# Expert index look-up in three wide VectorE instructions, and query-weight low parts moved from GpSimd to VectorE

## The chip, the cores and the metric

The kernel runs on one core of one Trainium2 chip. The metric is device time in microseconds (us): the median of three runs is 3392.26 us (3391.84 to 3396.86). In the profile PE is the matrix engine (TensorE), PEld its weight loads, DVE is VectorE, ACT is ScalarE, POOL is GpSimd, and SP is the queue that issues most DMAs.

## The reference, cut to what matters

The program is a two-block transformer over 512 tokens of width 1024 in fp32. The first block mixes attention, a recurrent layer and a routed feed-forward layer; the second ends in a sparse feed-forward layer with 16384 experts, each a row `u` and a row `v` of 1024 numbers. Only that last layer is touched. For each of 8 heads it does this:

```python
q = (xb @ w_query).reshape(128, 8, 2, 128)
sc = einsum('thpd,hpkd->thpk', q, sub_keys)             # 2 x 128 scores per head
s_top, i_top = top_k(sc, 16)                            # for each of the two halves
cand = s_top[:, :, 0, :, None] + s_top[:, :, 1, None, :]
cand_idx = i_top[:, :, 0, :, None] * 128 + i_top[:, :, 1, None, :]
best, pos = top_k(cand, 16)                             # 16 ranks out of the pair sums
eidx = take_along_axis(cand_idx, pos, axis=-1)          # <- the look-up
g = softmax(best)
h = gelu(einsum('thkd,td->thk', expert_u[eidx], xb))
out = einsum('thk,thkd->td', g * h, expert_v[eidx])
```

## The kernel before

The last phase (`phase_d`, L1064) has four stretches: a norm, the query stage (`d_query`, L1177), the gates (`d_gates`, L1245) and a main loop over 128 blocks of 128 experts (L1132).

*Query stage.* A loop over 8 groups g, one for each head. For each group two blocks of query weights (`wq`, 128x1024) are loaded. Each is split by `split` (L1053): ScalarE rounds it to the matrix engine's format (`wqh`, L1058), and an engine given as `eng` makes the low part `wql` = `wq` - `wqh` (L1061). Before the change that engine is GpSimd, with one buffer for `wqh` and one for `wql`. TensorE does 24 matmuls for each block (L1192), ScalarE copies the result (`qT`, L1194), 8 small matmuls (L1201) make the scores `sc`, and VectorE takes the top 16 of each row with five instructions of `top16` (L1285); GpSimd turns the found indices into floats (`it`, `pos`, L1294). VectorE adds the pair sums (`cd`) and GpSimd makes the matching expert numbers (`ci`), 50 candidates a token (L1216, L1218). A second `top16` gives `best` and `pos`. Then comes the look-up, L1222 to L1227: for each of 4 token tiles and 16 ranks, one VectorE instruction compares a row 0 to 49 with the rank's position, multiplies by `ci` and sums along the row into `ei`. The chip runs it as two instructions, the operation and the reading of the accumulator.

*Work beside it.* `h_step` (L1080) makes expert scores for one block of 128 experts: a load `uraw`, a split into `uh` (ScalarE) and `ul` (GpSimd, 128x1024, L1061), 24 matmuls (L1088), and a GELU `G` on ScalarE. In the code the first 33 of these (LA, L1066 and L1105) stand behind the gates. They need nothing of the query stage.

*Gates and main loop.* `d_gates` needs `ei` and the softmax of all groups. It builds a dense weight table with 768 matmuls, shared between VectorE, GpSimd and ScalarE, and stores it as `w_d`. The main loop reads it back as `wb`, and in each step does 18 matmuls (L1146), one later `h_step`, and gathers and sums for the last 128 tokens.

*Order.* Each engine runs its own queue in order. The order in each queue is made when the program is built, by a planner that simulates the timeline with a cost for each instruction (L1307). Only the VectorE queue of the main loop is in the order of the code (L1131). So the instructions of several groups, and `h_step` blocks, stand interleaved in the queues.

Of the kernel before, what the change touches and what calls it, by code (L numbers as in the profile page):

```python
# [5 lines left out]
F32 = mybir.dt.float32  # L6
# [4 lines left out]
OP = mybir.AluOpType  # L11
AX = mybir.AxisListType
# [11 lines left out]
NCAND = len(CANDS)  # L24
# [133 lines left out]
class K:  # L158
# [1018 lines left out]
    def d_query(self, dq, ps, hh, hl):  # L1177
        nc, I, X, C = self.nc, self.I, self.X, self.C
        sub = dq.tile([128, 16, 128], F32, name="sub")
        nc.sync.dma_start(sub, I["subk"])  # L1180
        best = dq.tile([128, 4, 8, 16], F32, name="best")
        for g in range(8):
            qT = dq.tile([128, 2, 512], F32, name="qT", bufs=2)
            for j in range(2):
                w = dq.tile([128, 8, 128], F32, name="wq", bufs=3)
                nc.sync.dma_start(w.rearrange("p k c -> p (k c)"), I["w_q"][2 * g + j])
                wh, wl = self.split(dq, "wq", w, [128, 8, 128], bufs=1, eng=nc.gpsimd)
                p = ps.tile([128, 512], F32, name="pj", tag="pj")
                n = 0
                for k in range(8):  # L1190
                    for l, r in ((wh, hh), (wh, hl), (wl, hh)):
                        nc.tensor.matmul(p, l[:, k, :], r[:, k, :], start=(n == 0), stop=(n == 23))  # L1192
                        n += 1
                nc.scalar.copy(qT[:, j, :], p)  # L1194
            st = dq.tile([128, 4, 2, 16], F32, name="st", bufs=2)
            it = dq.tile([128, 4, 2, 16], F32, name="it", bufs=2)
            for half in range(2):
                p = ps.tile([128, 2, 2, 128], F32, name="psc", tag="tr")
                for t in range(2):
                    for j in range(2):  # L1200
                        nc.tensor.matmul(p[:, t, j, :], qT[:, j, (2 * half + t) * 128:(2 * half + t) * 128 + 128],  # L1201
                                         sub[:, 2 * g + j, :], start=True, stop=True)
                sc = dq.tile([128, 2, 2, 128], F32, name="sc", bufs=2)
                nc.scalar.copy(sc, p)
                for t in range(2):
                    for j in range(2):
                        self.top16(dq, sc[:, t, j, :], st[:, 2 * half + t, j, :], it[:, 2 * half + t, j, :], 128)
            cd = dq.tile([128, 4, NCAND], F32, name="cd", bufs=2)
            ci = dq.tile([128, 4, NCAND], F32, name="ci", bufs=2)
            i1 = dq.tile([128, 4, 16], F32, name="i1", bufs=2)  # L1210
            nc.gpsimd.tensor_scalar(i1, it[:, :, 0, :], 128.0, None, op0=OP.mult)
            for a, b2, dst, eng in ((st[:, :, 0, :], st[:, :, 1, :], cd, nc.vector), (i1, it[:, :, 1, :], ci, nc.gpsimd)):
                o = 0
                for i in range(8):
                    n = 16 // (i + 1)
                    eng.tensor_add(dst[:, :, o:o + n], b2[:, :, 0:n], a[:, :, i:i + 1].to_broadcast([128, 4, n]))  # L1216
                    o += n
                eng.tensor_add(dst[:, :, o:o + 8], a[:, :, 8:16], b2[:, :, 0:1].to_broadcast([128, 4, 8]))  # L1218
            pos = dq.tile([128, 4, 16], F32, name="pos", bufs=2)
            for t in range(4):  # L1220
                self.top16(dq, cd[:, t, :], best[:, t, g, :], pos[:, t, :], NCAND)
            for t in range(4):  # L1222
                for k in range(16):
                    eq = dq.tile([128, NCAND], F32, name="eq", bufs=2)
                    nc.vector.scalar_tensor_tensor(eq, C("iota")[:, 0:NCAND], pos[:, t, k:k + 1], ci[:, t, :],
                                                   op0=OP.is_equal, op1=OP.mult,
                                                   accum_out=self.ei[:, t, g * 16 + k:g * 16 + k + 1])  # L1227
        eu, ev = self.eix
        nc.vector.tensor_copy(eu, self.ei[:, 3, :])
        hi = dq.tile([128, 128], I32, name="ehi")  # L1230
        nc.vector.tensor_scalar(hi, eu, 7, None, op0=OP.logical_shift_right)
        nc.vector.tensor_scalar(ev, eu, 127, None, op0=OP.bitwise_and)
        nc.vector.tensor_scalar(ev, ev, 7, None, op0=OP.logical_shift_left)
        nc.vector.tensor_add(ev, ev, hi)
        bf = best.rearrange("p t h k -> p (t h) k")
        g3 = self.gt.rearrange("p t (h k) -> p (t h) k", h=8)
        nc.vector.tensor_sub(g3, bf, bf[:, :, 0:1].to_broadcast([128, 32, 16]))
        nc.scalar.activation(g3, g3, AF.Exp)
        sm = dq.tile([128, 32], F32, name="smg")
        nc.vector.tensor_reduce(sm, g3, axis=AX.X, op=OP.add)  # L1240
        nc.vector.reciprocal(sm, sm)
        nc.vector.tensor_mul(g3, g3, sm.unsqueeze(2).to_broadcast([128, 32, 16]))
        nc.gpsimd.tensor_copy(self.g3, self.gt[:, 3, :])
# [67 lines left out]
```

## Time and profile before

| | |
|---|---|
| median of the runs | 3392.26 us |
| span of the profiled execution, first to last instruction | 3389.1 us |
| median less span | 3.2 us |
| TensorE busy in the span | 3087.1 us (91%) |
| VectorE | 1869.1 us (55%) |
| ScalarE | 972.4 us (29%) |
| GpSimd | 1147.7 us (34%) |
| mean granted TensorE clock | 0.966 |

The page gives the span of the profiled execution, and no other time of its own. An engine's busy time is the union of its instructions' times. One instruction's recorded time can overlap that of the next on the same engine, so mean times are longer than the distance from start to start. The shares are averages over very different stretches of the program; the stretch that the change touches runs from about 1996 to 2310 us of the span.

### The profile page before, as it was taken

The page shows a single profiled execution, that of the slowest core. Times are in us where ns is not written, and L with a number is a line of the kernel's source. Part 1 is how long each engine was busy: PE and PEld are TensorE (multiplying, and loading weights), DVE is VectorE, ACT ScalarE, POOL GpSimd, SP SyncE. Part 2 cuts the span into 40 slices and gives each one's busy share as a digit, 9 for nine tenths or more (in the row PEclk, how much of TensorE's full clock was granted, in tenths as well). Part 3 has the DMA queues.
Part 4 walks back from the last instruction along what each step waited for, and adds up shares of the span by engine and source line. Part 5 has one row for each costly group of instructions (what it writes and reads, how often), then busy time and mean ns, then how long its engine had stood idle before and what let it go on. Part 6 is the DMA issues. An engine that isn't in the chain of part 4 may idle for free. (4 is left out here: it accounts for less than half of the span.)

```text
span 3389.1 us, 43135 instructions
## 1 busy us (share of the span) xinstructions
PE 3087.1 (91%) x16081; PEld 2175.6 (64%) x16081; DVE 1869.1 (55%) x4502; ACT 972.4 (29%) x1745; POOL 1147.7 (34%) x979
## 2 busy tenths in 40 slices
PE   7999999978988888888879998878889999999998
PEld 6777776463323323333356677767779999999986
DVE  2456665460000000000043649999979988898978
ACT  3333333220000000000033642226833333333332
POOL 0433321010000000000012134447858877777743
PEclk9999999989999999999988999988999999999999
DMA  4221112488999999999931252215788888888877
GB/s 145 100 73 60 57 67 85 136 322 349 428 426 427 427 428 426 427 427 428 420 103 64 69 171 82 69 57 165 206 305 314 314 292 306 300 300 303 291 258 265
DMA packets 193358, 837.91 MB, mean 247 GB/s; under 512 B 16509, under 2 KB 66301, under 8 KB 168446
## 3 DMA queue, kind: packets, MB, share of 16 engines
q1 hardware_dynamic: 153230, 693.52, 53.4%
q0 software_dynamic: 38592, 140.53, 11.8%
q8 instruction: 127, 2.08, 0.2%
q10 hardware_dynamic: 1328, 1.11, 0.1%
q14 instruction: 81, 0.66, 0.1%
HBM read 794.47 MB, written 40.63 MB: 246 GB/s over the span
## 5 line engine op out<-in xcount | busy, mean ns | idle before, releaser
L876 DVE TENSOR_TENSOR sg<-sg,pu 128x512 f32<-128x512 f32 x32 | 22.0, 687 | 681.9 <-PE pu L872 681.9
L1061 POOL TENSOR_TENSOR ul<-uraw,uh 128x1024 fp32r<-128x1024 f32 x128 | 333.4, 2606 | 124.6 <-ACT uh L1058 123.2
L1088 PE MATMUL ph<-hTh,ul 128*128 128x384 f32 x1024 | 347.9, 340 | 20.7 <-POOL ul L1061 20.7
L1088 PE MATMUL ph<-hTh,uh 128*128 128x384 f32 x1024 | 348.5, 341 | 0.4 <-ACT G L1091 0.4
L1088 PE MATMUL ph<-hTl,uh 128*128 128x384 f32 x1024 | 348.0, 340 | 0.0
L1146 PE MATMUL pY<-vh,ah 128*128 128x512 f32 x768 | 302.5, 394 | 20.3 <-ACT ah L1058 20.3
L1146 PE MATMUL pY<-vl,ah 128*128 128x512 f32 x768 | 300.4, 391 | 0.0
L872 PE MATMUL pu<-wt,xeT 128*64 128x512 f32 x1024 | 259.9, 611 | 33.5 <-DMA wt<-in_wu_dram 33.5
L1146 PE MATMUL pY<-vh,al 128*128 128x512 f32 x768 | 278.3, 389 | 0.0
L872 PE MATMUL pg<-wt,xeT 128*64 128x512 f32 x1024 | 256.4, 610 | 21.2 <-DMA wt<-in_wg_dram 21.2
L885 PE MATMUL pd<-wt,aT 128*64 128x512 f32 x1024 | 245.2, 597 | 22.6 <-ACT aT L881 22.6
L306 PE MATMUL pj<-hh,wh 128*128 128x512 f32 x528 | 216.0, 409 | 1.8 <-DVE hl L205 1.1
L306 PE MATMUL pj<-hh,wl 128*128 128x512 f32 x528 | 217.2, 411 | 0.0
L306 PE MATMUL pj<-hl,wh 128*128 128x512 f32 x528 | 215.0, 407 | 0.0
L853 POOL DMA_INDIRECT xe<-h_d,idi x8 | 7.6, 955 | 612.2 <-PE pt L859 578.9
L1088 PEld LDWEIGHTS ph<-hTh,ul 128*128 128x128 f32 x1024 | 194.6, 190 | 23.5 <-POOL ul L1061 23.1
L872 PEld LDWEIGHTS pu<-wt,xeT 128*64 128x64 f32 x1024 | 85.7, 141 | 192.3 <-issue 145.3
L1058 ACT CAST vh<-vraw 128x1024 fp32r<-128x1024 f32 x128 | 134.6, 1051 | 258.9 <-PE pY L1146 212.9
L872 PEld LDWEIGHTS pg<-wt,xeT 128*64 128x64 f32 x1024 | 86.5, 140 | 180.4 <-issue 148.0
L1088 PEld LDWEIGHTS ph<-hTh,uh 128*128 128x128 f32 x1024 | 195.0, 191 | 5.7 <-ACT G L1091 1.1
L1088 PEld LDWEIGHTS ph<-hTl,uh 128*128 128x128 f32 x1024 | 194.9, 190 | 4.4
L885 PEld LDWEIGHTS pd<-wt,aT 128*64 128x64 f32 x1024 | 89.5, 136 | 151.0 <-issue 120.2
(434 smaller groups left out, 6287.0 us busy)
## 6 DMA issues: line engine op xcount, KB each, us to landing
wt<-in_wg_dram SPq DMA_DIRECT2D x64, 2048.0 KB
wt<-in_wu_dram SPq DMA_DIRECT2D x64, 2048.0 KB
wt<-in_wd_dram SPq DMA_DIRECT2D x64, 2048.0 KB
uraw<-in_put_dram SPq DMA_DIRECT2D x128, 512.0 KB
vraw<-in_pv_dram SPq DMA_DIRECT2D x128, 512.0 KB
wraw<-in_w_in_dram SPq DMA_DIRECT2D x32, 1024.0 KB
w_d<-wst SPq DMA_DIRECT2D x12, 2048.0 KB
wb<-w_d SPq DMA_DIRECT2D x32, 768.0 KB
```

The source lines that it names most:

```text
L306: nc.tensor.matmul(p, l[:, k, :], r[:, k, :], start=(i == 0), stop=(i == 23))
L853: nc.gpsimd.indirect_dma_start(out=xe, out_offset=None, in_=h_d, in_offset=bass.IndirectOffsetOnAxis(ap=idi[:, p:p + 1], axis=0))
L872: nc.tensor.matmul(dst[e * 64:e * 64 + 64], xT[:, k, e * 64:e * 64 + 64], ww[e][:, k, :], start=(k == 0), stop=(k == 7))
L876: nc.vector.tensor_mul(sg, sg, pu)
L885: nc.tensor.matmul(pd[h][e * 64:e * 64 + 64], aT[:, k, e * 64:e * 64 + 64], wd[e][:, k, h * 512:h * 512 + 512], start=(c == 0 and k == 0), ...
L1058: nc.scalar.copy(hi, src)
L1061: (eng or nc.vector).tensor_sub(lo, src, hi)
L1088: nc.tensor.matmul(p, l[:, k, :], r[:, k, 0:ND], start=(n == 0), stop=(n == 23))
L1146: nc.tensor.matmul(pY[t][h], l[:, t * 128:t * 128 + 128], r[:, h * 512:h * 512 + 512], start=(s == 0 and n == 0), stop=(s == 127 and n == 2))
```

## The change

The look-up of one token tile is done for all 16 ranks at once, over a tile of 16x50: a comparison of the row 0 to 49 (repeated for each rank) with the 16 positions (each repeated 50 times), a product with `ci` (repeated for each rank), and a sum along the last axis. The tile `eq` has one buffer of 800 floats a partition, where it had two of 50. Second, the low parts `wql` are made by the default engine of `split`, VectorE, and `wqh` and `wql` have two buffers each.

```diff
@@ d_query, for each of 8 groups and 2 blocks
-                wh, wl = self.split(dq, "wq", w, [128, 8, 128], bufs=1, eng=nc.gpsimd)
+                wh, wl = self.split(dq, "wq", w, [128, 8, 128], bufs=2)
@@ d_query, for each of 8 groups
             for t in range(4):
-                for k in range(16):
-                    eq = dq.tile([128, NCAND], F32, name="eq", bufs=2)
-                    nc.vector.scalar_tensor_tensor(eq, C("iota")[:, 0:NCAND], pos[:, t, k:k + 1], ci[:, t, :],
-                                                   op0=OP.is_equal, op1=OP.mult,
-                                                   accum_out=self.ei[:, t, g * 16 + k:g * 16 + k + 1])
+                eq = dq.tile([128, 16, NCAND], F32, name="eq")
+                nc.vector.tensor_tensor(eq, C("iota")[:, None, 0:NCAND].to_broadcast([128, 16, NCAND]),
+                                        pos[:, t, :].unsqueeze(2).to_broadcast([128, 16, NCAND]), op=OP.is_equal)
+                nc.vector.tensor_mul(eq, eq, ci[:, t:t + 1, :].to_broadcast([128, 16, NCAND]))
+                nc.vector.tensor_reduce(self.ei[:, t, g * 16:g * 16 + 16], eq, axis=AX.X, op=OP.add)
```

## Rows read from the trace of the kernel before

**Rows 1.** Stretches (us from:to, length): busy PE, PEld, DVE, ACT, POOL; clock, DMA, GB/s.
```profile
2024.00:2310.00 286.00, 230.58 (x1132) 207.03 (x1130) 284.44 (x1880) 73.83 (x104) 131.24 (x219) 0.91 0.22 71
2310.00:2464.00 154.00, 120.20 (x849) 108.36 (x848) 131.73 (x466) 121.49 (x320) 135.29 (x202) 0.93 0.69 201
2464.00:3389.00 925.00, 911.41 (x4512) 815.96 (x4512) 814.41 (x775) 325.99 (x441) 629.46 (x340) 0.99 0.84 296
```
**Rows 2.** VectorE, 2024 to 2310: busy us, mean ns, idle before, releaser.
```profile
L1225 DVE SCALAR_TENSOR_TENSOR eq<-con,pos,ci 128x50 f32<-128x50 f32 x512 | 183.4, 398 | 0.7 <-POOL ci L1218 0.7
```
**Rows 3.** Line L1225: ns least, median, most; first and last start.
```profile
L1225 DVE SCALAR_TENSOR_TENSOR eq<-con,pos,ci x512: 169/259/2531, 2040.3 to 2307.2; 128x50 f32<-128x50 f32 x171
L1225 DVE DVE_READ_ACCUMULATOR eq<-con,pos,ci x512: 70/76/84, 2042.7 to 2307.4; 128x1 f32 x171
```
**Rows 4.** Timeline, VectorE (start, us): first and last of 16 looks.
```profile
2117.51 0.26 DVE L1225 SCALAR_TENSOR_TENSOR eq<-con,pos,ci 128x50 f32<-128x50 f32 x1
...
2120.38 0.26 DVE L1225 SCALAR_TENSOR_TENSOR eq<-con,pos,ci 128x50 f32<-128x50 f32 x1
```
**Rows 5.** Timeline, VectorE, 2104 to 2114 us.
```profile
2104.23 2.33 DVE L1225 SCALAR_TENSOR_TENSOR eq<-con,pos,ci 128x50 f32<-128x50 f32 x1
...
2111.80 0.20 DVE L1290 FIND_INDEX8 iu<-best,cd 128x8 uint32<-128x50 f32 x1
...
2112.10 1.86 DVE L1225 SCALAR_TENSOR_TENSOR eq<-con,pos,ci 128x50 f32<-128x50 f32 x1
```
**Rows 6.** Timeline, GpSimd, the same stretch.
```profile
2104.09 2.40 POOL L1061 TENSOR_TENSOR ul<-uraw,uh 128x1024 fp32r<-128x1024 f32 x1
...
2111.55 2.34 POOL L1061 TENSOR_TENSOR wql<-wq,wqh 128x1024 fp32r<-128x1024 f32 x1
```
**Rows 7.** GpSimd groups, 2024 to 2310.
```profile
L1061 POOL TENSOR_TENSOR ul<-uraw,uh 128x1024 fp32r<-128x1024 f32 x27 | 64.2, 2380 | 6.6 <-ACT uh L1058 6.6
L1061 POOL TENSOR_TENSOR wql<-wq,wqh 128x1024 fp32r<-128x1024 f32 x13 | 30.7, 2364 | 0.0
```
**Rows 8.** Timeline, VectorE: instructions of 512 elements, and a next one.
```profile
2281.37 0.68 DVE L1240 TENSOR_REDUCE smg<-gt 128x32 f32<-128x512 f32 x1
...
2282.91 0.68 DVE L1242 TENSOR_TENSOR gt<-gt,smg 128x512 f32<-128x512 f32 x1
2283.51 0.26 DVE L1225 SCALAR_TENSOR_TENSOR eq<-con,pos,ci 128x50 f32<-128x50 f32 x1
```
**Rows 9.** Timeline, VectorE: low parts of 1024 elements, two and one.
```profile
1962.49 2.36 DVE L1061 TENSOR_TENSOR wol<-wo,woh 128x1024 fp32r<-128x1024 f32 x2 [0.85 <-ACT woh L1058]
1965.19 1.22 DVE L1061 TENSOR_TENSOR wol<-wo,woh 128x1024 fp32r<-128x1024 f32 x1 [0.34 <-ACT woh L1058]
```
**Rows 10.** Timeline, VectorE: an instruction and the next, which reads its result.
```profile
2307.54 0.23 DVE L1229 CAST eix<-ei 128x128 int32<-128x128 f32 x1
2307.80 0.23 DVE L1231 TENSOR_SCALAR ehi<-eix 128x128 int32<-128x128 int32 x1
```
**Rows 11.** Waits, 1996 to 2310: total us, times, longest.
```profile
PE pj L1192 <- POOL wql L1061: 32.9, 10, 5.6
DVE st L1289 <- ACT sc L1204: 31.5, 1, 31.5
```
**Rows 12.** Timeline, ScalarE: second weight block, its result, the first scores.
```profile
2005.72 1.05 ACT L1058 CAST wqh<-wq 128x1024 fp32r<-128x1024 f32 x1 [4.32 <-issue]
2006.67 0.58 ACT L1194 COPY qT<-pj 128x512 f32<-128x512 f32 x1
...
2018.61 0.58 ACT L1194 COPY qT<-pj 128x512 f32<-128x512 f32 x1
...
2023.49 0.58 ACT L1204 COPY sc<-psc 128x512 f32<-128x512 f32 x1 [2.29 <-PE psc L1201]
```
**Rows 13.** Timeline, TensorE: first and last of 22 query matmuls in a row.
```profile
2012.52 0.39 PE L1192 MATMUL pj<-hTh,wql 128*128 128x512 f32 x1
...
2017.41 0.40 PE L1192 MATMUL pj<-hTh,wql 128*128 128x512 f32 x1
```

## The prediction

> **What bounds the kernel now.** Read the busy times by stretch first [rows 1]. There the reader sees which engine is full in each stretch. VectorE has waited 31.5 us for the first scores [rows 11]. From 2024 to 2310, the query stage, VectorE is busy 284.4 of 286.0 us, and TensorE 230.6 at a granted clock of 0.91: VectorE sets the end, and the expert-score blocks (`h_step`) that stand interleaved fill TensorE. The gates, 2310 to 2464, need `ei` of all groups. They load all of VectorE, GpSimd and ScalarE, and the change does not touch them. In the main loop TensorE is busy 911.4 of 925 us. So the path runs through VectorE for 286 us, through the gates, and through TensorE to the end; a microsecond off the query stage moves all that follows by one, as long as TensorE still gets its blocks done before it.
>
> The second view is the group of the look-up line inside that stage [rows 2, 3]. Its 512 instructions have a median of 259 ns, a mean of 398 and a most of 2531. A mean so far over the median asks for the third view, the timeline. Undisturbed, a pair (operation and accumulator reading) starts every (2120.38 - 2117.51)/15 = 0.191 us [rows 4]. The long ones end where a GpSimd split ends: 2104.23 + 2.33 = 2106.56 beside 2104.09 + 2.40 = 2106.49, and 2112.10 + 1.86 = 2113.96 beside 2111.55 + 2.34 = 2113.89 [rows 5, 6]. FIND_INDEX8, with one large input, runs in 0.20 us inside the same GpSimd split. So a look-up, which reads two SBUF tensors, stands still while GpSimd runs a split. That time is (398 - 259) x 512 = 71 us. The line's VectorE time is then 512 x 0.191 = 98 us of work and 71 us of holds, 169 in all. From the first top-16, when the first scores are copied (2023.49 + 0.58 = 2024.1, [rows 12]), to the end of the look-up at 2307.5 [rows 3] are 283.4 us, so everything else (top-16, pair sums) takes 114.
>
> **The change, part by part.** *Look-up removed:* 98 us of work, and its exposure to holds. *Look-up added:* 32 tiles x 3 = 96 instructions of 800 elements. No row has 800. One of 512 takes 0.68 us, as a sum or as a product whose second input repeats along the row [rows 8], one of 1024 takes 1.22 [rows 9]; on the line between them 800 takes 0.98. The next instruction starts 0.08 before the recorded end if it is independent (2283.51 - 2282.91 = 0.60 against 0.68), and 0.03 after it if it reads the result (2307.80 - 2307.54 = 0.26 against 0.23) [rows 8, 10]. Comparison, product and sum depend on each other in turn and `eq` has one buffer, but the planner can put another group's top-16 between. So each costs 0.90 to 1.01, together 86 to 97 us; I take 92, the middle.
>
> The Trainium skill ("VectorE: DVE Perf Modes", the section on the TRN2 errata) says that each SBUF instruction pays a fixed extra latency, so that a few large tiles beat many small ones. By the recorded durations that looks right here, 0.335 us for a pair of 50 elements; by the starts it is not, since a pair follows the last after 0.191 us. By the rule the look-up would give far more than by the row; that is the fourth rival below.
>
> *Low parts of the query weights:* 16 splits of 1024 come onto VectorE at 2.36/2 = 1.18 us [rows 9], 18.9 us. From GpSimd go 16 of 2.36 us, 38 us, 13 of them inside VectorE's stage [rows 7]. GpSimd is busy 131 of 286 us there [rows 1], so its own relief is worth nothing; what counts is that 13 of 40 holders go.
>
> *Holds left:* 27 splits `ul` stay [rows 7]. Today each of the 40 costs 71/40 = 1.8 us of its 2.37, since a two-input instruction starts every half microsecond. After the change 64 wide ones, 16 splits and 72 pair sums start in some 260 us, one every 1.7 us; a split then runs on average 0.9 us before it is met and costs 1.5. That makes 27 x 1.5 = 40 us. The sum along the row has one input, like FIND_INDEX8, and should not be held. The bounds are 0.6 each (a split mostly meets top-16 alone), 16 us, and the whole 2.4, 65 us; I take 40, nearest to today's row.
>
> *Second buffer for `wqh` and `wql`:* today the rounding of the next block waits until the matmuls of the last have read the only buffer. At the start the second block is rounded only at 2005.72, its result comes at 2018.61 and the first scores at 2023.49 [rows 12]. A block's 24 matmuls take 24 x (2017.41 - 2012.52)/21 = 5.6 us [rows 13]. With two buffers the second result can follow the first (2006.67) after that, at 2012.3, so 6 us earlier. Nothing if the planner keeps `h_step` blocks between; 8 at most. I take 6.
>
> *Waits added:* the low parts now stand in VectorE's in-order queue among top-16 and look-ups, and TensorE waits for them there instead of 32.9 us for GpSimd [rows 11]. Behind a late one stand the 24 matmuls, `qT`, and the next group's scores. I cost this at nothing because TensorE's results come well ahead: VectorE waits for scores only once, 31.5 us at the start [rows 11]. If that cover goes, the first rival holds. The DMAs and SP's queue issue the same loads; no load is added.
>
> *Sum:* the stage becomes 114 + 92 + 19 + 40 = 265 us against 283, 18 less, and starts 6 earlier: 24 us. TensorE is busy 231 of the stage's 286 us [rows 1], so it can give 55 before it is the end itself. The profiled span is 3389.1 us, 3.2 below the median of the runs; both should move alike: 3392.3 - 24 = 3368 us. The kernel's look-up by itself hardly gains (98 against 92, less than the 19 that come on); the gain is in the holds and the start. With the bounds: best 114 + 86 + 19 + 16 = 235 and 8 at the start, 56 less, 3336; worst 114 + 97 + 19 + 65 = 295 and no earlier start, 12 more, 3404.
>
> **Rivals.** *1. Starved groups (slower).* The planner queues both low parts of group g+1 behind the last look-up of group g. Then VectorE stands idle each time for that group's results: two blocks' matmuls, 11.2 us [rows 13], and two copies of 0.58 [rows 12] make 12.4; with the score matmuls between them some 13 us (at the start, with `h_step` blocks between, it was 2023.49 - 2005.72 = 18). For 7 groups 91 us, less 24: 3459. It decides as soon as idle before `st` exceeds 3 us a group. Against it: low parts need only a load and a rounding, are ready early, and have two buffers; only one wait for scores is there today.
>
> *2. Turns between the two engines (not faster).* A wide instruction holds GpSimd for 0.98 us where a short one held it for 0.2. The `ci` sums and position casts then come late, the product waits for them, and each released GpSimd split holds the next product in full. At 4.4 us a group more than summed this takes 35 us: 3403. From 3 us a group the gain is gone. For it: no planner cost shows such holds. Against it: VectorE waited for `ci` only 0.7 us in the whole stage [rows 2]. The Trainium skill ("SBUF — State Buffer", "Who interferes with whom") has the rule for both directions: whichever of the two issues first keeps the shared port for the whole instruction. The rows above show one direction; no row before shows a wide one holding GpSimd.
>
> *3. Blocks pushed out.* The planner puts fewer `h_step` blocks into a shorter stage; each one that lands in the gates costs GpSimd 2.38 us [rows 7], where it is busy 135 of 154 [rows 1]. Seven cost 17: 3385.
>
> *4. Durations count, not starts.* 512 x (0.259 + 0.076) = 171 us [rows 3] against 96 x 0.98 = 94 gives 77 instead of 6: 95 less, 3297. Against it: by that count, with 71 us of holds, the line would hold 243 us, and it was busy 183.4 [rows 2].
>
> **How the numbers follow.** Forecast 0.60, rival 1 0.09, rival 2 0.14, rival 3 0.12, rival 4 0.05. About 0.2% (7 us) is what a measurement of this kernel can tell. Faster: the forecast nearly whole (0.59), half of rival 3, and rival 4: 0.70. Within: 0.01 of the forecast, half of rival 3, 0.06 of rival 2: 0.13. Slower: rival 1 and the rest of rival 2: 0.17. The range 3338 to 3400 leaves out rivals 1 and 4 and a little at both ends, under 0.2; the forecast's own range is 3338 to 3385.
>
> **What would show it.** Right: VectorE's stage some 265 us long and still full; 96 wide instructions of 0.9 to 1.0 us from start to start where undisturbed; comparisons and products, not sums, stretched to 2 us and ending with a `ul`; no `wql` on GpSimd; first top-16 near 2018. Wrong: idle on VectorE before `st` in each group (rival 1), products waiting for `ci` or `pos` (rival 2), more than five `ul` after the last look-up (rival 3), or a main loop that does not start earlier by what the stage saved.

## The result: 3338.7 us, faster by 1.6%, over twice the forecast

The changed kernel takes 3338.72 us (median of four, 3335.2 to 3341.98) against 3393.55 us beside it: ratio 0.9841, 95% interval 0.9827 to 0.9855, or 54 us less. The forecast was 24 less, 3368. The direction and the place were right, the size was not. The profiled execution took 3341.98 us, with a span of 3340.2; the span of before was 3389.1, so the two traces differ by 49 us; the profiled execution is the slowest of the four, which is why the medians differ by more.

The stretches of the changed kernel, cut where its own stages begin and end, with the columns of [rows 1]:

```profile
1996.00:2019.00 23.00, 22.60 (x111) 18.91 (x110) 5.82 (x5) 11.12 (x15) 4.97 (x2) 1.00 0.56 192
2019.00:2258.00 239.00, 219.72 (x1160) 200.89 (x1159) 237.34 (x952) 72.23 (x103) 136.02 (x207) 0.99 0.25 84
2258.00:2414.00 156.00, 121.03 (x858) 110.25 (x857) 136.97 (x477) 122.07 (x322) 136.54 (x203) 0.93 0.68 200
2414.00:3340.00 926.00, 911.52 (x4512) 816.92 (x4512) 815.42 (x775) 325.66 (x441) 632.17 (x340) 0.99 0.83 295
```

The reader sees the whole gain in the first two lines: VectorE's stage, first top-16 to last look-up, is 239 us where it was 283, and starts 5 us earlier; gates and main loop have kept their lengths. VectorE is still full, 237.3 of 239. TensorE does 1160 matmuls in 219.7 us at a granted clock of 0.99; in [rows 1] it did 1132 in 230.6 at 0.91.

The look-up's groups in that stage (busy us, mean ns, idle before), which answer to [rows 2], and the least, median and most of its first two instructions, which answer to [rows 3]:

```profile
L1226 DVE TENSOR_TENSOR eq<-eq,ci 128x800 f32<-128x800 f32 x32 | 44.4, 1389 | 0.3 <-POOL ci L1218 0.2
L1224 DVE TENSOR_TENSOR eq<-con,pos 128x800 f32<-128x800 f32 x32 | 36.9, 1152 | 0.2
L1227 DVE TENSOR_REDUCE ei<-eq 128x16 f32<-128x800 f32 x32 | 31.1, 972 | 0.1
```
```profile
L1226 DVE TENSOR_TENSOR eq<-eq,ci x32: 967/981/3047, 2038.4 to 2256.3; 128x800 f32<-128x800 f32 x32
L1224 DVE TENSOR_TENSOR eq<-con,pos x32: 964/979/2095, 2036.3 to 2254.3; 128x800 f32<-128x800 f32 x32
```

Mean over median gives the holds again: (1152 - 979) x 32 = 5.5 us and (1389 - 981) x 32 = 13.1. The sum L1227, with one input, has none (972). One hold of a comparison on the timeline, VectorE and then GpSimd:

```profile
2109.80 0.96 DVE L1227 TENSOR_REDUCE ei<-eq 128x16 f32<-128x800 f32 x1
...
2111.48 1.88 DVE L1224 TENSOR_TENSOR eq<-con,pos 128x800 f32<-128x800 f32 x1
2113.28 0.08 DVE L1291 MATCH_VALUE_LOAD s<-st,sc 128x8 f32 x1
```
```profile
2110.10 2.40 POOL L1061 TENSOR_TENSOR ul<-uraw,uh 128x1024 fp32r<-128x1024 f32 x1
2112.45 0.96 POOL L1294 CAST it<-iu 128x16 f32<-128x16 uint32 x1
```

The split starts at 2110.10. VectorE works 1.4 us on under it, on the sum and on top-16, before it meets the comparison at 2111.48; that one is held until 2112.5 and then runs its 0.9. The GpSimd cast behind the split takes 0.96 us instead of 0.20: it ends 0.05 us after the comparison. So holds go both ways.

For every kernel below I summed, over VectorE's instructions from the first top-16 to the last look-up, the distance from each start to the next. An undisturbed look-up is 98 us of work in the narrow form and 86 in the wide one (32 x (0.889 + 0.889 + 0.884), the least distances); an undisturbed set of pair sums is 6.5. What lies above, the low parts' excess over 1.12 us each included, is holds: in the changed kernel 19 us on the look-up and 10 on the pair sums. "Splits" are GpSimd's 2.4 us subtractions within the stage.

| kernel | ratio, 95% interval | stage us | look-up | pair sums | low parts | splits | holds | per split |
|---|---|---|---|---|---|---|---|---|
| before | 1 | 283.4 | 168.9 | 9.1 | 0 | 40 | 73 | 1.8 |
| changed | 0.9841 [0.9827, 0.9855] | 239.1 | 104.5 | 16.8 | 12.4 | 30 | 29 | 0.96 |
| second buffer alone | 0.9987 [0.9976, 0.9998] | 276.4 | 162.8 | 8.9 | 0 | 39 | 67 | 1.7 |
| low parts alone (VectorE, two buffers) | 0.9961 [0.9947, 0.9976] | 278.9 | 155.7 | 6.6 | 12.5 | 30 | 58 | 1.9 |
| wide look-up alone | 0.9890 [0.9873, 0.9906] | 251.5 | 130.7 | 10.9 | 0 | 41 | 49 | 1.2 |
| wide, VectorE, one buffer | 0.9870 [0.9849, 0.9891] | 247.8 | 111.1 | 11.2 | 17.4 | 30 | 33 | 1.1 |
| wide, GpSimd, two buffers | 0.9850 [0.9833, 0.9866] | 234.5 | 113.3 | 15.4 | 0 | 40 | 36 | 0.9 |

### The profile page after: what moved, and what is told of

The parts are those of the page before. It is cut to its first block, busy times and chain, and to the rows that moved or that the text cites. A ratio compares the mean times of both kernels' runs of the same rounds, so it can differ in the third digit from the quotient of the medians.

```text
span 3340.2 us, 42188 instructions
## 1 busy us (share of the span) xinstructions
PE 3072.6 (92%) x16081; PEld 2166.9 (65%) x16081; DVE 1834.3 (55%) x3590; ACT 970.9 (29%) x1745; POOL 1144.9 (34%) x963
## 4 chain that ended last, share of the span: by engine, by line
PE 71%; DMA 13%; DVE 11%; ACT 3%; issue 1%; POOL 1%; SPq 0%; DVEq 0%; ACTq 0%; POOLq 0%
PE pY L1146 14%; PE ph L1088 13%; PE pj L306 11%; DMA wt<-in_wu_dram 8%; PE pu L872 5%; PE pd L885 5%; PE pg L872 5%; DMA wt<-in_wg_dram 3%; PE pout L769 2%; PE po L897 2%; PE pj L468 1%; PE pq L626 1%; PE pw L1280 1%; DVE eq L1226 1%; DVE o L1278 1%
## 5 line engine op out<-in xcount | busy, mean ns | idle before, releaser
L1061 POOL TENSOR_TENSOR ul<-uraw,uh 128x1024 fp32r<-128x1024 f32 x128 | 340.8, 2663 | 130.5 <-ACT uh L1058 128.9
```

Source lines behind the costliest of these rows:

```text
L1061: (eng or nc.vector).tensor_sub(lo, src, hi)
```

## Experiments

The diffs of second buffer alone and low parts alone are against the kernel before, the others of the next part against the changed kernel; `...` marks lines that are left out.

**The parts one by one.** The theory after the result, H: what counts is how long one GpSimd split holds VectorE, and the wide form halves that. The rival R: the second buffer changes the order of the queues, and the order makes the gain. In the changed kernel all 16 query-weight blocks do stand ahead of nearly all `h_step` blocks in TensorE's queue (two to three of these start before the last query block); with one buffer they alternate, two to three `h_step` blocks to a group.

*Wide look-up alone* (low parts on GpSimd, one buffer):

```diff
-                wh, wl = self.split(dq, "wq", w, [128, 8, 128], bufs=2)
+                wh, wl = self.split(dq, "wq", w, [128, 8, 128], bufs=1, eng=nc.gpsimd)
```

> The wide look-up alone; low parts of the query weights on GpSimd with one buffer, as before. The changed kernel's VectorE stage is 239 us against 283: start to start, the 96 wide instructions take 86 us against 98 for the narrow ones, and holds by GpSimd splits fall from 75 to 28 us. Theory H (holds per split): a GpSimd split stops a wide look-up for 0.94 us on average where it stopped a narrow one for 1.8 to 1.9, because single-input work stands between the wide ones. 40 splits x 0.94 = 38 us of holds, no low parts on VectorE: 12 + 37 = 49 us less than before, about 3344. Rival R (order): the gain comes from the second buffer, which lets all query matmuls run before the expert-score blocks; here that order is the old one, so only the 12 us of look-up work go: about 3381.

Measured: 3359.55 against 3395.05, 37 us less by the ratio. R, which left 12 us, falls; H, with 49, is right in kind and too large, since a split still held 1.2 us.

*Low parts alone:*

```diff
-                wh, wl = self.split(dq, "wq", w, [128, 8, 128], bufs=1, eng=nc.gpsimd)
+                wh, wl = self.split(dq, "wq", w, [128, 8, 128], bufs=2)
```

> Low parts of the query weights on VectorE with two buffers; the look-up rank by rank as before. H: 27 or 28 splits remain at 1.9 us = 53 us of holds against 75, 22 less; 12 of the low parts' 18 us stand inside the stage; the first top-16 starts 5 us earlier: about 15 us less than before, 3378. R: the order is that of the changed kernel, so most of its 55 us come: 3345 to 3360.

Measured: 3380.87, 13 us less. H was 15. TensorE's order here is that of the changed kernel, and R's 35 to 50 did not come.

*Wide look-up, low parts on GpSimd, two buffers:*

```diff
-                wh, wl = self.split(dq, "wq", w, [128, 8, 128], bufs=2)
+                wh, wl = self.split(dq, "wq", w, [128, 8, 128], bufs=2, eng=nc.gpsimd)
```

> Wide look-up, low parts on GpSimd as before but with two buffers for each part. H: as the wide look-up alone with a start 5 us earlier, 40 splits at 0.94: about 54 us less, 3339, level with the changed kernel. The prediction's own reason (13 holders gone from GpSimd) would make it 10 to 20 us slower than the changed kernel: 3350 to 3360. R: as the changed kernel, 3339.

Measured: 3346.14, 51 us less; the interval overlaps that of the changed kernel. The prediction said that "13 of 40 holders go" is what counts. Here all 40 stay, and the look-up ends at the same time (2257.5 us in this trace, 2258.3 in the changed kernel's). With the wide look-up that reason is refuted.

*Second buffer alone:*

```diff
-                wh, wl = self.split(dq, "wq", w, [128, 8, 128], bufs=1, eng=nc.gpsimd)
+                wh, wl = self.split(dq, "wq", w, [128, 8, 128], bufs=2, eng=nc.gpsimd)
```

> Two buffers for each part and nothing else: low parts on GpSimd, look-up rank by rank. H: 5 us from the earlier start, 40 splits still cost 1.8 each: 3388. R: the query matmuls run before the expert-score blocks, as in the changed kernel, and most of the gain is there: 3345 to 3360.

Measured: 3391.21, 4 us less, as H said. The stage itself ends 5.5 us earlier, counted from the last residual sum of the phase before, but in this trace it takes 168 us from the last look-up to the main loop, where it took 160 before. The order alone is worth next to nothing while the look-up is narrow.

*The changed kernel with one buffer:*

```diff
-                wh, wl = self.split(dq, "wq", w, [128, 8, 128], bufs=2)
+                wh, wl = self.split(dq, "wq", w, [128, 8, 128], bufs=1)
```

> The changed kernel with one buffer for each part of the query weights (wide look-up, low parts on VectorE). The first four runs: wide look-up alone 36 us less than before, with a second buffer 49 to 51, the second buffer alone 4. Theory H2: the buffer decides where the expert-score blocks stand in TensorE's queue; with one they are spread over the whole stage and each GpSimd split holds a wide look-up 1.2 us, with two they stand behind the query matmuls and cost about 1.0. Here 28 splits x 1.2 = 35 us of holds, 15 of low parts on VectorE, 85 of wide look-up, 112 of the rest: stage 248 against 283, about 3358. Rival (the prediction's reason: fewer splits on GpSimd are what pays): as the changed kernel, 3340.

Measured: 3351.13, 44 us less. The stage is 247.8 us, as H2 had it (248), with 1.1 us a split. With a wide look-up the second buffer is thus worth some 10 us here (the two intervals just overlap) and 14 between the two kernels with low parts on GpSimd; with a narrow one it is worth 4. The holds do get cheaper with it: after its start a split meets the first two-input instruction of VectorE 1.0 us later on average with one buffer, and 1.3 to 1.4 us later with two. Why it does is not shown: no run moves a split against the look-up by itself.

**The holds taken away.** The same edit in the changed kernel and in the one before; the low parts of the first 33 `h_step` blocks are left out:

```diff
-                uh, ul = self.split(d1, "u", u, [128, 8, 128], eng=nc.gpsimd)
+                if s < LA:
+                    uh = d1.tile([128, 8, 128], F32R, name="uh", bufs=2)
+                    ul = d1.tile([128, 8, 128], F32R, name="ul", bufs=2)
+                    nc.scalar.copy(uh, u)
+                    nc.gpsimd.memset(ul.rearrange("p k e -> p (k e)").bitcast(F32), 0.0)
+                else:
+                    uh, ul = self.split(d1, "u", u, [128, 8, 128], eng=nc.gpsimd)
```

> The changed kernel, but the low parts of the first 33 expert-score blocks are left out: GpSimd writes zeros in their place (a memset, which reads nothing), so those blocks' low-part products are of zeros. H: the 28 to 30 us of holds vanish; wide comparisons and products take 0.89 us each from start to start. VectorE's stage would be 210 us, but TensorE, busy 222 of 239 us there, becomes the end: 15 to 20 us less than the changed kernel, about 3322. Rival (a memset holds as a subtraction does, the port is not it): 3339.

> The kernel before, with the same left out: zeros by a memset in place of the low parts of the first 33 expert-score blocks; the query weights' low parts stay on GpSimd. H: 27 of 40 holders stop holding the narrow look-ups; 27 x 1.8 = 49 us off a stage of 283: about 3345, with the 13 query splits still seen as look-ups of 2 us. Rival (holds are not what fills the line): 3390.

Measured: the changed kernel 3312.89 (ratio to before 0.9766, 0.9745 to 0.9788), the one before 3344.45 (0.9850, 0.9828 to 0.9871). The second is the purest proof: 51 us by taking the reading out of 27 GpSimd instructions, without touching VectorE's code; its look-up fell from 169 to 116 us, and the query splits still show: each of the 12 look-ups over 0.6 us stands beside a split, and 56 run wholly under a memset, none of them over 0.27 us. Below are its narrow look-up (ns least, median, most), then the wide products and comparisons of the other kernel (busy us, mean ns, idle before), and that kernel's memsets:

```profile
L1231 DVE SCALAR_TENSOR_TENSOR eq<-con,pos,ci x512: 160/256/2491, 2045.7 to 2259.2; 128x50 f32<-128x50 f32 x171
```
```profile
L1232 DVE TENSOR_TENSOR eq<-eq,ci 128x800 f32<-128x800 f32 x32 | 31.3, 977 | 0.1
L1230 DVE TENSOR_TENSOR eq<-con,pos 128x800 f32<-128x800 f32 x32 | 31.2, 975 | 0.2
```
```profile
L1087 POOL MEMSET ul<- 128x1024 f32 x29 | 27.7, 954 | 14.7 <-PE ph L1094 14.6
```

In the changed kernel without these splits no wide instruction is long: mean 975 to 977, the look-up 86.0 us, the stage 210.8, VectorE's work and nothing else. TensorE was not yet the end at 211 us, so the expectation's 3322 was too cautious. A memset is also shorter than a split, 0.95 us against 2.4; but 17 of the 33 memsets run beside a comparison or product, and none of these takes over 1.0 us, so it is not a shorter hold but none. The Trainium skill ("SBUF — State Buffer", "Who interferes with whom") says that a VectorE instruction with two SBUF inputs contends with a GpSimd instruction that reads SBUF and not with one that only writes; both traces agree, with 29 memsets of 0.95 us among 975 ns products in one and look-ups of at most 0.27 us under memsets in the other.

**Size of the look-up.** Four ranks at once:

```diff
+                for r in range(0, 16, 4):
-                eq = dq.tile([128, 16, NCAND], F32, name="eq")
+                    eq = dq.tile([128, 4, NCAND], F32, name="eq")
...
+                    nc.vector.tensor_reduce(self.ei[:, t, g * 16 + r:g * 16 + r + 4], eq, axis=AX.X, op=OP.add)
```

> The changed kernel with the look-up done for 4 ranks at once: 384 instructions of 200 elements instead of 96 of 800. Work by the fixed 0.056 us and 1.042 ns an element: 0.264 x 384 = 101 us against 85. Theory S (starts: a split runs until the next two-input instruction starts): two-input ones start every 0.75 us, so 28 splits x 2.0 = 56 us of holds, stage 112 + 101 + 12 + 56 = 281: about 3380. Theory T (share: what counts is how much single-input time VectorE can put under a split, and that share is the same): 1.0 each, 29 us, stage 254: about 3355.

Measured: 3405.22 against 3395.18, ratio 1.0036 (1.0019 to 1.0052): slower than the rank-by-rank form. Theory T (a split costs what it did in the 16-rank form) falls: instructions held for over 0.3 us lose 54 us, as S had it (56: a split lasts until the next two-input instruction starts). And a second cost comes that neither had; the stage is 313.7 us where S had 281. On VectorE's timeline near the end of the stage:

```profile
2291.77 0.37 DVE L1227 TENSOR_TENSOR eq<-eq,ci 128x200 f32<-128x200 f32 x1
2292.17 0.36 DVE L1228 TENSOR_REDUCE ei<-eq 128x4 f32<-128x200 f32 x1
2292.56 0.37 DVE L1225 TENSOR_TENSOR eq<-con,pos 128x200 f32<-128x200 f32 x1
```

Comparison, product and sum follow each other with nothing between, and each starts 0.03 us after the recorded end of the last: 0.40 from start to start, where 0.26 was the least. The last top-16 of this kernel ran at 2285 us, the last look-up at 2326: for 41 us there was nothing left to put between. Over the whole stage 245 of the 384 instructions are followed only after their recorded end; at 0.14 us each that is 33 us. The kernel loses only 12, since the stage starts 6 us earlier and 36 whole `h_step` blocks stand ahead of the gates: 151 us to the main loop instead of 160. In the 16-rank form it is 8 of 96, and the median distance is 0.89, 0.09 less than the duration: there the planner had other work for nearly every gap. This form has one `eq` buffer; four ranks with two were not run.

Eight ranks at once, with two `eq` buffers, and two PSUM buffers a tag in the query stage (the gates in a pool of their own with three):

```diff
+                for r in range(0, 16, 8):
+                    eq = dq.tile([128, 8, NCAND], F32, name="eq", bufs=2)
...
-            with tc.tile_pool(name="dk", bufs=1) as dk, tc.tile_pool(name="kps", bufs=3, space=PSUM) as ps:
...
+                with tc.tile_pool(name="kps", bufs=2, space=PSUM) as ps:
+                with tc.tile_pool(name="gps", bufs=3, space=PSUM, reuse_waits="tile") as ps, \
```

> The changed kernel with the look-up done for 8 ranks at once (192 instructions of 400 elements, two buffers), and the query stage's matrix results in 2 instead of 3 PSUM buffers a tag (the gates keep 3, from a pool of their own). It is the control of the next run. Work 0.47 x 192 = 90 us against 86. Holds by a GpSimd split were 1.8 us with 512 narrow look-ups, 1.9 with 384 of 200 elements, 0.96 with 96 wide ones; by the distance between two-input starts (1.2 us) about 1.4 here: 30 x 1.4 = 42. Stage 111 + 90 + 12 + 42 = 255 against 239: about 3355. If two buffers hide what the single buffer shows: 3345.

Measured: 3371.61, ratio 0.9924 (0.9901 to 0.9947), stage 268.5 against an expected 255; the look-up took 131 us. A split held 1.6 us, not the 1.4 expected. So the wide form needs its width: 12 us slower than before with 4 ranks, 26 faster with 8 (in other PSUM pools), 54 with 16.

**No second SBUF input.** As the eight-rank form, with `eq` and the row 0 to 49 in PSUM:

```diff
-                    eq = dq.tile([128, 8, NCAND], F32, name="eq", bufs=2)
-                    nc.vector.tensor_tensor(eq, C("iota")[:, None, 0:NCAND].to_broadcast([128, 8, NCAND]),
+        iop = ps.tile([128, NCAND], F32, name="iop", bufs=1)
+        nc.vector.tensor_copy(iop, C("iota")[:, 0:NCAND])
...
+                    eq = ps.tile([128, 8, NCAND], F32, name="eq", bufs=1)
+                    nc.vector.tensor_tensor(eq, iop[:, None, :].to_broadcast([128, 8, NCAND]),
```

> As the 8-rank control, but the row 0 to 49 and the tile eq lie in PSUM (one bank each, eq with one buffer), so that no look-up instruction reads two SBUF tensors. H (a GpSimd split holds only VectorE instructions with two SBUF inputs): comparisons, products and sums run undisturbed under the splits, holds are left on pair sums and query splits alone, 8 to 10 us; PSUM may cost up to 0.1 us an instruction (19 us), taken as 10: stage 111 + 90 + 12 + 9 + 10 = 232, about 3332. Rival (any VectorE instruction with two inputs is held): as the control, 3355, or later by what PSUM costs.

Measured: 3331.93, ratio 0.9821 (0.9804 to 0.9837): 35 us under its control, the eight-rank form, by the ratios, and at H's 3332. The products of the control and then of this kernel (ns least, median, most):

```profile
L1229 DVE TENSOR_TENSOR eq<-eq,ci x64: 544/560/2772, 2049.1 to 2294.1; 128x400 f32<-128x400 f32 x64
```
```profile
L1231 DVE TENSOR_TENSOR eq<-eq,ci x64: 551/568/583, 2042.6 to 2252.2; 128x400 f32<-128x400 f32 x64
```

None is held. Where the operand lies decides, not that there are two.

*Sixteen ranks, in two PSUM banks* (pools as in the eight-rank form):

```diff
+        eqp = ps.tile([128, 2, 512], F32, name="eqp", bufs=1)
+        eq = eqp[:, :, 0:8 * NCAND].rearrange("p b (k c) -> p b k c", c=NCAND)
+        iop = eqp[:, 1, 448:448 + NCAND]
...
```

> The changed kernel with the wide look-up of 16 ranks kept, but eq and the row 0 to 49 in PSUM (two banks), query stage with 2 PSUM buffers a tag. H: the look-up is not held: 96 x 0.9 = 86 us (the 8-rank PSUM form took 100 with nothing longer than undisturbed); pair sums and query splits hold 8 us: stage 111 + 86 + 12 + 8 = 217 against 239, about 3318, the best so far. Rival (an instruction across two PSUM banks is slower, or TensorE, busy 222 us of the changed kernel's stage, becomes the end): 3330.

Measured: 3325.54, ratio 0.9793 (0.9772 to 0.9815): the fastest that does all the work; its interval lies below that of the changed kernel. Its products, and one of them inside a GpSimd split (VectorE, then GpSimd):

```profile
L1232 DVE TENSOR_TENSOR eqp<-eqp,ci x32: 975/994/1022, 2046.9 to 2243.5; 128x800 f32<-128x800 f32 x32
```
```profile
2131.59 0.99 DVE L1232 TENSOR_TENSOR eqp<-eqp,ci 128x800 f32<-128x800 f32 x1
```
```profile
2130.12 2.40 POOL L1061 TENSOR_TENSOR ul<-uraw,uh 128x1024 fp32r<-128x1024 f32 x1
```

The longest of 32 is 1022 ns; none is held. The stage is 220.6 us against the 217 of H, with TensorE busy 212.7 of the 216 from 2019 to 2235: the next bound is near. The first top-16 comes 45.2 us after the last residual sum of the phase before, not 40.4 as in the changed kernel, so the time lies between H's 3318 and its rival's 3330.

*The same with low parts on GpSimd:*

```diff
-                wh, wl = self.split(dq, "wq", w, [128, 8, 128], bufs=2)
+                wh, wl = self.split(dq, "wq", w, [128, 8, 128], bufs=2, eng=nc.gpsimd)
```

> As the 16-rank PSUM form, but with the query weights' low parts on GpSimd again (two buffers). H: once the look-up can't be held, low parts on GpSimd cost VectorE nothing, and its 12 us of low-part work go: 3306, or 3315 if TensorE is then the end. Rival (the prediction's reason, each split leaving GpSimd pays): slower than the form with low parts on VectorE, 3325 or more.

Measured: 3331.09, ratio 0.9810 (0.9790 to 0.9829); the two intervals overlap. VectorE's stage did get 10 us shorter, 211.0, as H said. But in TensorE's queue 31 whole `h_step` blocks stand ahead of the gates' matmuls instead of 35, and from the last look-up to the main loop's first matmul it takes 169 us instead of 156: given back later, the way of rival 3. That stretch with low parts on VectorE, then on GpSimd, with the columns of [rows 1]:

```profile
2245.00:2401.00 156.00, 118.15 (x831) 105.74 (x830) 135.32 (x479) 121.98 (x321) 132.66 (x202) 0.93 0.70 204
```
```profile
2239.00:2408.00 169.00, 132.26 (x926) 120.62 (x924) 141.03 (x479) 128.08 (x329) 141.21 (x206) 0.94 0.67 200
```

The same holds over all the kernels here: with 31 whole blocks ahead of the gates this stretch takes 168 to 169 us, with 33 or 34 it takes 159 to 163, with 36 it takes 149 to 152. So each block more that is done before goes with 3 to 4 us less there. Which engine sets that was not separated.

*Low parts of the first 33 `h_step` blocks on VectorE too* (in the changed kernel):

```diff
-                uh, ul = self.split(d1, "u", u, [128, 8, 128], eng=nc.gpsimd)
+                uh, ul = self.split(d1, "u", u, [128, 8, 128], eng=nc.vector if s < LA else nc.gpsimd)
```

> The changed kernel with the low parts of the first 33 expert-score blocks made on VectorE as well, all other work kept. H: 29 us of holds go, 30 x 1.13 = 34 us of splits come onto VectorE: stage 244 against 239, about 3343; no look-up over 1 us. Rival (low parts leaving GpSimd are what pays, as the prediction has it for the query weights): each of 30 saves 0.4 us or more, 3326 or less.

Measured: 3337.38, ratio 0.9837 (0.9821 to 0.9854): the same as the changed kernel. In the stage the move does not pay: holds fall from 29 us to 6, 29 splits bring 33 us of work, and the stage is 248.2 us against 239.1 (H had 244). What follows gives it back: 36 whole blocks now stand ahead of the gates instead of 34, and the stretch from the last look-up to the main loop takes 149 us instead of 159. The rival's 3326 did not come.

## Why the prediction was wrong

The mechanism stood: GpSimd's splits hold two-input instructions of VectorE, the wide form is hardly less work, and VectorE sets the end. The step that failed is in the sum of the stage, 265 us against 239, and above all its term for the holds that are left:

- **"Holds left": 40 us, measured 29.** This is the largest of the mis-sized terms, 11 us. It lies within its stated bounds, 16 and 65; the value taken was too high. I let a split run until the next of "64 wide ones, 16 splits and 72 pair sums", one every 1.7 us, so 0.9 us on average. But these do not start at even distances: only 11 of the 16 splits are in the stage, and the 72 pair sums stand in 32 runs of one to eight. Of the 30 GpSimd splits 4 met no two-input instruction that started under them, and the other 26 met the first after 1.4 us on average (0.4 in the kernel before); until then VectorE worked on, on sums and top-16. Per split 0.96 us was lost, not 1.5. The price of 1.8 for the narrow form was right: leaving 27 readers out gave 51 us, against 27 x 1.8 = 49.
- **"Low parts of the query weights": 19 us, measured 12.4.** 11 of the 16 lie inside the stage; the first five ran while VectorE still waited for scores. The 1.18 us each was 1.13 from start to start.
- **"Look-up added": 92 us, measured 86 undisturbed.** The best bound was the truth: 0.89 each, because for 88 of the 96 the planner found other work to put behind. Four ranks show what happens when it does not.
- **"Everything else": 114 us, measured 111.** The 114 held 2.6 us of holds on pair sums, which the 40 counts again. The four terms together are the 26 us by which the stage was put too long.
- **Start: 6 us earlier, measured 5.** The first top-16 comes 40.4 us after the last residual sum of the phase before, where it was 45.2.
- "What counts is that 13 of 40 holders go" was the wrong reason for a right sign. With the wide look-up the engine of the low parts makes no measurable difference (0.9850 against 0.9841), since 7 us fewer holds and 12 us more work make the stage 5 us longer, and a first top-16 that comes 4 us earlier pays that. With the narrow look-up the move is worth some 9 us (0.9987 to 0.9961).
- The parts do not add: the second buffer gives 4 us, the wide look-up 37, both 51. The remainder, 10 us, belongs to neither alone. On top of the wide look-up the buffer takes away 13 us of holds (49 to 36), 4 of waits and 2 at the start, and costs 5 up to the main loop: 32 whole blocks stand ahead of the gates instead of 34.
- "A microsecond off the query stage moves all that follows by one" held in the changed kernel, where 34 whole blocks stand ahead of the gates and 33 did before. It did not hold where that number moved by more, as above.

Rival 1 did not come: no wait of VectorE for `st` of any length is in the trace. Rival 2 did not decide: the hold of GpSimd is there (casts `pos` at a mean of 480 ns instead of 196), but VectorE waited only 0.2 us for `ci`. Rival 3 did not come in this kernel: 34 whole blocks stand before the gates, and 33 stood there before. It came with the second buffer alone (31) and with `eq` in PSUM and low parts on GpSimd (31). Rival 4 is refuted by 0.89 us from start to start.

## What to carry to other kernels

When one instruction form has a mean far above its median, look at what the other engines were doing at the long ones before counting instructions: 71 of this look-up's 169 us were GpSimd reading SBUF. There are three cures here: make the two-input instructions few and wide, with single-input work between them (37 us alone); put one operand in PSUM so that only one comes from SBUF (35 us with eight ranks; 16 with sixteen, in other PSUM pools; not run with the narrow form); move the reader off GpSimd, which pays only as long as the moved work is less than the holds (some 9 us with the narrow form, nothing measurable with the wide one). A wide form pays only with other work to fill its dependent chain; cut into quarters, with one `eq` buffer, it was slower than 512 narrow instructions. And look at what the shorter stage no longer covers: work that it leaves over can take the gain back in the next one.

## What the runs showed that was not expected

- A single-input conversion can be held too. Right after the stage, in the changed kernel, VectorE and GpSimd:

```profile
2261.18 0.29 DVE L1253 CAST f_i<-a_i 128x256 f32<-128x256 int32 x1
2264.32 5.33 DVE L1253 CAST f_i<-a_i 128x256 f32<-128x256 int32 x1 [1.98 <-PE ptr L1256]
```
```profile
2263.85 0.94 POOL L1110 DMA_INDIRECT X<-in_pu_dram,eix  x1 [0.30 <-issue]
2264.82 4.68 POOL L1061 TENSOR_TENSOR ul<-uraw,uh 128x1024 fp32r<-128x1024 f32 x2
```

The same cast takes 0.29 us alone and 5.33 where it starts under the issue of a gather and two splits follow; it ends 0.15 us after them. The cast `eix` just before takes 1.30 us, where it took 0.23 in the kernel before [rows 10], and also ends with a split. The sums and top-16 were never seen held: the longest were 1.03 and 0.34 us.

- A product of 800 elements with `eq` in PSUM and across two banks costs 994 ns in the median, 981 in SBUF.
- TensorE's granted clock was 1.00 (2.4 GHz) from 2019 to 2104 us, where the query matmuls keep it busy without a pause (85.0 of 85.0 us), and 0.99 over the stage; before it was 0.91 in the mean, with TensorE busy 230.6 of 286.0 us [rows 1]. Low parts alone has the same order of query matmuls and 0.93 from 2019 to 2298 (233.7 of 279.0 us busy), so the order by itself does not give it. No run here moves the clock alone.
